# Two-layer DiT block in fp32 on one core: modulation steps of the FFN two to a tile, three chunks moved to layer 1's projections, later stores, a second norm row buffer, early first splits of the down projection

## The chip, the cores and the metric

The kernel runs on one core of a Trainium2 chip. A time is the device time of one execution, in microseconds; of several runs the median is given. PE is TensorE, DVE VectorE, ACT ScalarE, POOL GpSimd, and SP is SyncE, which here issues nearly all transfers.

## The reference, cut to what matters

Two layers over 1024 tokens and 256 context tokens of width 1024, all in fp32. Layer 0 mixes a gated recurrence with an attention over latent keys, layer 1 is a differential attention. Around them:

```python
for li in range(2):
    mod = silu(c) @ w_mod[li] + b_mod[li]
    mod_c = silu(c_ctx) @ w_mod[li] + b_mod[li]
    sh1, sc1, ga1, sh2, sc2, ga2 = split(mod, 6)
    u = rmsnorm(h, g_norm1[li]) * (1 + sc1) + sh1
    y, yc = mixer(u, uc)
    h = h + ga1 * y
    u = rmsnorm(h, g_norm2[li]) * (1 + sc2) + sh2
    a, g = split(u @ w_up[li], 2)
    h = h + ga2 * ((gelu(dwconv(g)) * a) @ w_down[li])
    # layer 0 does the same for the context with mod_c
```

## The kernel before, in words

Every fp32 product is three matmuls of rounded parts, hi·hi, lo·hi and hi·lo (`mm3`, L116 to L118). An operand is split by an ACT copy (L283, hi) and a DVE subtraction (L98, lo), for some weights by POOL instead (L90). The stages in order, with their places in the span: layer 0's front and mixer to about 740, its output projection (`out_proj`) to 857, the start of its FFN (`begin0`, `up_sequence`) to 909, the up projection's tiles to 1492.6, the down projection (`ffn_down`) to 1845.6, layer 1's projections (`layer1_front`) to 2185, the differential attention, output projection 1 to 2717, layer 1's up projection to 3177 and its down projection to the end.

**Modulation.** The 12 columns of 512 of `w_mod` of a layer are chunks. A chunk in `mod_chunk_dve` is a generator of six steps that other code calls one at a time: (1) POOL clears the sum, `b_mod` is loaded into its first row, the first 512 KB piece of `w_mod` is requested; (2) to (5) DVE adds two products of that piece per context (L194, `macc<-wr,sc,macc`; four instructions with two contexts, two with one), and SP requests the next piece into the same single buffer; (6) PE sums over the partitions with matmuls one column wide (`modps`, L204, or L211 for the gates) and DVE copies the result out.

**Up projection** (`up_sequence`). The 2816 hidden columns are 22 tiles of 128; a tile is a seven-product scheme over halves of the operands (products "11", "t2", "t1", "t3", "21", "t4", "22" into the PSUM banks B, E, A, and C for the context). The order of the code is the order of the engines here. In each pass the previous tile is finished: DVE takes the gate, convolves it (L930 to L932), multiplies it by the other half (L1118, `gc`) and SP stores it in `hid` (L1119). `some_mods()` runs a modulation step in one slot after product t1 (a second one there, if there are more than two a tile) and one after `second(X)`. The last piece of a chunk is thus added in the first slot and summed by PE in the second. Layer 0 has nine chunks here: four and two of two contexts, three of one.

**Down projection** (`ffn_down`). Rounds of 4, 3 and 3 token tiles (layer 1: 4 and 4), 22 items a round, one for each 128 hidden columns. An item's weights `wr` and hidden rows `hr` are requested three items ahead (`fetch`), split one item ahead (`split`) and multiplied into `acc`. At a round's end DVE multiplies `acc` by the gate `ga` (L1235, `dtmp`) and POOL adds it to the residual (L1236). One extra step per item or so follows: in layer 0's rounds 1 and 2 the 18 steps of chunks 7 to 9 of layer 1, then the norm of finished token tiles for layer 1 (`columns`, three steps each: Square on ACT with the rstd chain of POOL's pow and DVE's L130 to L133; PE's transposes `ntp` with DVE's and ACT's `v`; the split to `u`).

**Output projection.** Items are staggered: load, product, and the norm some items later, in one row buffer `xn`, which takes the Square's output first and the normed row later, and which PE's transposes read.

**Layer 1's projections.** 56 items (block, token tile) in the block order 4, 2, 3, 0, 1, 5, staggered with lags; here a planner places instructions by its own time model within each engine's queue. Three token tiles that the down projection leaves are loaded, scaled (lag 4) and normed (lag 7) early. Blocks 0 to 3 end with a norm, the rotation and four transposes whose result goes out as `dk` or `dq` (L1336, 128 KB each).

## Time and profile before

| | us |
|---|---|
| median of 3 runs | 3421.39 |
| lowest and highest run | 3420.65, 3423.81 |
| the profiled execution's own time | 3431.7 |
| its span | 3429.9 |
| PE, DVE, ACT, POOL busy | 3186.3, 2360.9, 1412.1, 945.2 |
| mean granted clock of PE | 0.974 |

Times in rows count from the span's start. A table of stretches gives for each stretch its length, each engine's busy time with its instructions, then the granted clock of PE (1.00 is the level of 2.4 GHz, 0.5 that of 1.2 GHz, between them a mixture), the busy share of the DMA engines and GB/s. In a timeline the bracket tells how long the engine was idle before the row, and what released it. A wait row reads: engine, what waited, what it waited for, then the total, the times and the longest.

### The profile page before, as it was taken

To read this page: it belongs to the slowest core of one execution; us is meant where nothing else is said; L and a number is where in the kernel's file an instruction comes from. 1 tells how busy PE (TensorE), PEld (TensorE's weight loads), DVE (VectorE), ACT (ScalarE), POOL (GpSimd) and SP (SyncE) were. 2 spreads that over 40 slices of the span, in tenths; PEclk is the share of its full clock that TensorE was granted. 3 is DMA by queue.
4 is the path that set the end of the run, shared out by engine and by line. 5 is a ranking of instruction groups with operands and counts; after the bars stand their busy time and mean duration, and the time that the engine had idled before them with its cause. 6 is when DMAs were issued, how large, how long until landed. Compare 5 with 4: busy or idle time off the path is not lost.

```text
span 3429.9 us, 43450 instructions
## 1 busy us (share of the span) xinstructions
PE 3186.3 (93%) x16262; PEld 2633.3 (77%) x16262; DVE 2360.9 (69%) x3381; ACT 1412.1 (41%) x2444; POOL 945.2 (28%) x654
## 2 busy tenths in 40 slices
PE   8998889989799999989899999888888889999998
PEld 4777778878578778868777887777777768888887
DVE  6468978855776777643566687599997687666443
ACT  3355766733422223322243222477763333333322
POOL 2223578864000000000122223277764200000010
PEclk9999999999899999999999999999999999999999
DMA  6224953344122223234755355444414122223553
GB/s 261 70 77 129 285 141 94 89 137 134 47 96 97 97 97 111 97 123 151 249 192 182 120 139 131 146 114 126 111 62 160 62 86 101 90 74 98 181 180 124
DMA packets 232298, 434.07 MB, mean 127 GB/s; under 512 B 21484, under 2 KB 147692, under 8 KB 230296
## 3 DMA queue, kind: packets, MB, share of 16 engines
q1 hardware_dynamic: 230216, 424.49, 39.3%
q10 hardware_dynamic: 1872, 6.82, 0.6%
q8 instruction: 128, 2.10, 0.2%
q14 instruction: 82, 0.67, 0.1%
HBM read 319.89 MB, written 111.34 MB: 126 GB/s over the span
## 4 chain that ended last, share of the span: by engine, by line
PE 54%; DVE 14%; DMA 3%; issue 3%; ACT 3%; POOL 1%; SPq 0%; DVEq 0%; ACTq 0%; POOLq 0%
PE acc L118 4%; PE pB L116 4%; PE pB L118 4%; PE pB L117 4%; PE acc L116 4%; PE acc L117 4%; DVE m L1456 3%; PE pj L116 3%; PE pj L117 3%; PE pj L118 3%; DVE p L1472 3%; PE pE L118 2%; PE pE L116 2%; PE pE L117 2%; PE ops L117 2%
## 5 line engine op out<-in xcount | busy, mean ns | idle before, releaser
L98 DVE TENSOR_TENSOR wl<-wr,wh 128x1024 fp32r<-128x1024 f32 (+2 forms) x285 | 348.8, 1233 | 92.9 <-ACT wh L283 63.4
L116 PE MATMUL acc<-wh,hh 128*128 128x512 f32 x792 | 312.5, 395 | 18.7 <-ACT wh L283 17.1
L118 PE MATMUL acc<-wl,hh 128*128 128x512 f32 x792 | 312.5, 395 | 9.6 <-DVE wl L98 8.9
L117 PE MATMUL acc<-wh,hl 128*128 128x512 f32 x792 | 310.6, 392 | 4.5 <-DVE hl L98 4.5
L1236 POOL TENSOR_TENSOR ht<-ht,dtmp 128x1024 f32<-128x1024 f32 x17 | 45.7, 2715 | 857.1 <-DVE dtmp L1235 857.1
L283 ACT CAST wh<-wr 128x1024 fp32r<-128x1024 f32 (+1 forms) x221 | 220.9, 1008 | 83.4 <-DVE wr L999 72.4
L98 POOL TENSOR_TENSOR wl<-wf,wh 128x1280 fp32r<-128x1280 f32 x64 | 221.9, 3468 | 106.3 <-ACT wh L1491 94.7
L1451 PE MATMUL S<-k,q 128*128 128x512 f32 (+1 forms) x768 | 197.8, 382 | 55.7 <-ACT p L1462 55.5
L116 PE MATMUL pB<-ht,wh 128*128 128x512 f32 x528 | 210.4, 398 | 16.5 <-ACT ht L283 6.5
L98 DVE TENSOR_TENSOR hl<-hr,hh 128x512 fp32r<-128x512 f32 (+1 forms) x110 | 76.0, 691 | 206.7 <-ACT hh L283 206.6
L118 PE MATMUL pB<-lt,wh 128*128 128x512 f32 x528 | 210.3, 398 | 2.2 <-DVE lt L98 2.0
L117 PE MATMUL pB<-ht,wl 128*128 128x512 f32 x528 | 209.5, 397 | 0.8 <-DVE wl L98 0.8
L194 DVE SCALAR_TENSOR_TENSOR macc<-wr,sc,macc 128x512 f32<-128x512 f32 x192 | 135.8, 748 | 105.2 <-DMA wr<-w_mod 104.1
L283 ACT CAST hh<-hr 128x512 fp32r<-128x512 f32 (+1 forms) x110 | 63.7, 579 | 325.0 <-PE acc L118 242.0
L1462 ACT ACTIVATE p<-S,m 128x1280 f32<-128x1280 f32 x128 | 170.8, 1334 | 60.6 <-DVE m L1456 57.5
L1456 DVE TENSOR_REDUCE m<-S 128x1 f32<-128x1280 f32 x128 | 187.1, 1479 | 6.2 <-PE S L1451 5.6
L116 PEld LDWEIGHTS acc<-wh,hh 128*128 128x128 f32 x792 | 149.8, 189 | 53.4 <-ACT wh L283 21.8
L177 POOL MEMSET macc<- 128x512 f32 x24 | 12.4, 526 | 636.8 <-PE modps L211 283.3
L118 PEld LDWEIGHTS acc<-wl,hh 128*128 128x128 f32 x792 | 149.7, 189 | 49.4 <-DVE wl L98 18.6
L1451 PEld LDWEIGHTS S<-k,q 128*128 128x128 f32 x768 | 124.9, 193 | 77.2 <-ACT p L1462 64.5
L116 PE MATMUL pj<-wh,u 128*128 128x512 f32 x448 | 177.6, 396 | 2.5 <-DVE qT L98 2.5
L117 PE MATMUL pj<-wh,u 128*128 128x512 f32 x448 | 178.0, 397 | 0.0
(414 smaller groups left out, 9178.3 us busy)
## 6 DMA issues: line engine op xcount, KB each, us to landing
wr<-ffn_down SPq DMA_DIRECT2D x110, 512.0 KB
wr<-ffn_up SPq DMA_DIRECT2D x90, 512.0 KB
wr<-w_mod SPq DMA_DIRECT2D x76, 512.0 KB
hid<-gc SPq DMA_DIRECT2D x44, 512.0 KB
k<-dk SPq DMA_DIRECT2D x14, 1280.0 KB
hr<-hid SPq DMA_DIRECT2D x66, 256.0 KB
wr<-w_in_c SPq DMA_DIRECT2D x24, 512.0 KB
mr<-w_mod SPq DMA_DIRECT2D x20, 512.0 KB
```

The lines of the kernel that those rows point to most:

```text
L98: e.tensor_tensor(out, x, hi.bitcast(F32), op=SUB)
L116: mm(out, a[0], b[0], start=start, stop=False, skip_group_check=onto)
L117: mm(out, a[1], b[0], start=False, stop=False, skip_group_check=onto)
L118: mm(out, a[0], b[1], start=False, stop=stop, skip_group_check=onto)
L177: nc.gpsimd.memset(acc[c], 0.0)
L194: nc.vector.scalar_tensor_tensor(acc[c], raw[:, kk * 512:(kk + 1) * 512], self.sc[:, 2 * u + kk, c:c + 1], acc[c], op0=MUL, op1=ADD)
L283: self.nc.scalar.copy(hi, x)
L1236: (nc.vector if last else nc.gpsimd).tensor_tensor(hts[t][:, c], hts[t][:, c], tmp[:, c], op=ADD)
L1451: nc.tensor.matmul(Y["S", m][:, c0:c0 + n], heads[h]["q"][m][:, t * P:(t + 1) * P], heads[h]["k"][x, m, j], start=(x == 0), stop=(x == 1))
L1456: nc.vector.tensor_reduce(Y["m", m], Y["S", m][:, :TOK], axis=AX.X, op=ALU.max, negate=True)
L1462: nc.scalar.activation(Y["p", m], Y["S", m][:, :TOK], AF.Exp, bias=Y["m", m], accum_out=Y["s"] if m else s0[:, h, t:t + 1])
L1472: nc.vector.scalar_tensor_tensor(Y["p", 0], Y["p", 1], Y["tt"], Y["p", 0], op0=MUL, op1=ADD)
```

## The change

1. `up_sequence`: two steps a tile, one in each slot; the third call goes. Layer 0's list has six chunks of two contexts (36 steps for 18 tiles); layer 1's chunks 4 to 6 leave it, 7 to 9 leave the down projection, and all six run in `layer1_front`, one step for each item outside block 4 (`mod`, lag 5).
2. The store of `hid` goes out after `second(X)`, half a tile later, but for the last tile.
3. `fetch_down` requests the first down item's operands in tile 20, and tile 21 splits them (`self.ahead`); `ffn_down` begins with them. The gate rows `ga` are requested at item 4.
4. `norm` in `out_proj` has two `xn` buffers. Room for it: one `cgc` buffer, a smaller DMA scratch, and W's split tiles all 1024 wide.
5. The start of the up projection splits "t2" before it copies out the first product (`p1_out`; in layer 1 there is nothing to copy).
6. In `layer1_front` the early scale and norm come one item later.

```diff
--- before.py
+++ after.py
@@ -828,7 +828,7 @@
...
-                xn = O.tile([P, D], F32, tag="xn", bufs=1, name="xn")
+                xn = O.tile([P, D], F32, tag="xn", bufs=2, name="xn")
                 junk = xn.rearrange("p (k c) -> p k c", c=P)
@@ -919,7 +919,7 @@
...
         n = x.shape[-1]
-        hi, lo = ((pool or self.W).tile([P, n], F32R, tag=tag + y, bufs=bufs, name="w" + y) for y in "hl")
+        hi, lo = ((pool or self.W).tile([P, n if pool else 1024], F32R, tag=tag + y, bufs=bufs, name="w" + y)[:, :n] for y in "hl")
         self.split(x, hi, lo)
@@ -946,7 +946,7 @@
...
         nc.scalar.copy(self.cg[:, 1:1 + CTX], pg)
-        gc = F.tile([P, CTX], F32, tag="cgc", bufs=2, name="gc")
+        gc = F.tile([P, CTX], F32, tag="cgc", bufs=1, name="gc")
         self.convolved(0, f, self.cg, gc, CTX)
@@ -1073,8 +1073,8 @@
...
         p1(X)
+        self.split_columns(U, "t2")
         p1_out(X)
-        self.split_columns(U, "t2")
         p6(X)
@@ -1101,7 +1101,6 @@
...
         mods += [x for ch in chunks for x in self.mod_steps(F, *ch)]
-        per = -(-len(mods) // (NF - 2))
         for f in range(1, NF + 1):
@@ -1116,8 +1115,8 @@
...
             nc.vector.tensor_mul(gc, gc, Y["sum"])
-            nc.sync.dma_start(self.hid_d[f - 1, :, :SEQ], gc)
             if f == NF:
+                nc.sync.dma_start(self.hid_d[f - 1, :, :SEQ], gc)
                 break
@@ -1127,8 +1126,6 @@
...
             some_mods()
-            if per > 2:
-                some_mods()
             if here:
@@ -1138,6 +1135,7 @@
...
             second(X)
+            nc.sync.dma_start(self.hid_d[f - 1, :, :SEQ], gc)
             some_mods()
@@ -1150,8 +1148,18 @@
...
                 raws = self.fetch_up(l, f + 2)
-        while mods:
-            some_mods()
+            elif f + 2 == NF:
+                raws = self.fetch_down(l)
+            else:
+
+                self.ahead = self.split_new(raws[1]), self.split_new(raws[0])
+        assert not mods
+
+    def fetch_down(self, l):
+        w, x = (self.W.tile([P, 1024], F32, tag="wr", bufs=NWR, name="wr") for _ in range(2))
+        self.nc.sync.dma_start(w, self.io["ffn_down"][l, :P, :])
+        self.nc.sync.dma_start(x[:, :512], self.hid_d[0, :, :512])
+        return w, x[:, :512]
@@ -1163,7 +1171,6 @@
...
             F = self.sb(st, f"down{l}")
-            gas = [self.ga(F, l, 1, c, f"ga{c}") for c in range(2 if l == 0 else 1)]
             extra = []
@@ -1196,9 +1203,9 @@
...
             with self.tc.manual_schedule():
-                for i in range(3):
+                parts[0] = self.ahead
+                for i in range(1, 3):
                     fetch(i)
-                split(0)
                 for r, tiles in enumerate(rounds):
@@ -1211,6 +1218,8 @@
...
                                 fetch(i + 3)
+                            if i == 4:
+                                gas = [self.ga(F, l, 1, c, f"ga{c}") for c in range(2 if l == 0 else 1)]
                             if f == 8:
@@ -1338,13 +1347,19 @@
...
                 self.heads = {}
+                mods = [step for ch in range(4, 10) for step in self.mod_steps(M, 1, ch, 1)]
+
+                def mod(item):
+                    if mods and item[0] != 4:
+                        mods.pop(0)()
...
                 early = (lambda f: lambda item: f(item[1] + n0) if item[0] == 4 and item[1] + n0 < NT else None)
-                self.staggered(items, (early(load), 0), (early(scale), 4), (early(norm), 7), (project, 4), (finish, 5), (first_head, 8))
+                self.staggered(items, (early(load), 0), (early(scale), 5), (early(norm), 8), (project, 4), (finish, 5), (mod, 5), (first_head, 8))
+                assert not mods
@@ -1628,10 +1643,10 @@
...
                     self.out_proj(0, "w_out_ab", [*range(NTX, NT), *range(NTX)], self.yT0, lambda: self.begin0(F0))
-                self.ffn_up(0, F0, [(1, ch, 2) for ch in range(4)] + [(0, ch, 2) for ch in (10, 11)] + [(1, ch, 1) for ch in range(4, 7)])
+                self.ffn_up(0, F0, [(1, ch, 2) for ch in range(4)] + [(0, ch, 2) for ch in (10, 11)] + [])
                 self.ctx_columns.close()
             columns = st.enter_context(ExitStack())
-            self.ffn_down(0, [range(0, 4), range(4, 7), range(7, NT)], lambda t: self.h1_d[t], range(7, 10), columns)
+            self.ffn_down(0, [range(0, 4), range(4, 7), range(7, NT)], lambda t: self.h1_d[t], (), columns)
             with ExitStack() as s2:
@@ -1708,7 +1723,7 @@
...
     arrays = layout({k: np.asarray(v) for k, v in inputs.items()})
-    nc = bacc.Bacc("TRN2", target_bir_lowering=False, num_devices=1, dynamic_dma_scratch_size=1024)
+    nc = bacc.Bacc("TRN2", target_bir_lowering=False, num_devices=1, dynamic_dma_scratch_size=512)
     io = {k: nc.dram_tensor(k, v.shape, F32, kind="ExternalInput").ap() for k, v in arrays.items()}
```

The order on SP where layer 0's up projection ends and its down projection begins, before:

```order
L1178 DMA wr<-ffn_down 128x1024
L1119 DMA hid<-gc 128x1024
L955 DMA hid<-gc 128x256
L1119 DMA hid<-gc 128x1024
L955 DMA hid<-gc 128x256
L1119 DMA hid<-gc 128x1024
L244 DMA ga<-ga_132 128x1024
L244 DMA ga<-ga_133 128x1024
L1181 DMA hr<-hid 128x512
L1178 DMA wr<-ffn_down 128x1024
L1181 DMA hr<-hid 128x512
```

and with the change:

```order
L915 DMA wr<-ffn_up 128x1024 x2
L1138 DMA hid<-gc 128x1024
L955 DMA hid<-gc 128x256
L1160 DMA wr<-ffn_down 128x1024
L1161 DMA wr<-hid 128x512
L1185 DMA wr<-ffn_down 128x1024
L1138 DMA hid<-gc 128x1024
L955 DMA hid<-gc 128x256
L1119 DMA hid<-gc 128x1024
L1188 DMA hr<-hid 128x512
```

The first down weights and hidden rows (L1160, L1161) now stand two tile stores ahead, the two `ga` loads are gone from here, and the request of item 1's rows (L1188) stands directly behind the last store.

DVE at the first items of round 1 of layer 0's down projection (`hl`, `wl` are an item's split rows and weights), before, from the round's end on, and one item later:

```order
L1235 TENSOR_TENSOR dtmp<-acc,ga 128x1024 x4
L98 TENSOR_TENSOR hl<-hr,hh 128x384
L98 TENSOR_TENSOR wl<-wr,wh 128x1024
L98 TENSOR_TENSOR hl<-hr,hh 128x384
L98 TENSOR_TENSOR wl<-wr,wh 128x1024
L194 SCALAR_TENSOR_TENSOR macc<-wr,sc,macc 128x512 x2
L98 TENSOR_TENSOR hl<-hr,hh 128x384
L98 TENSOR_TENSOR wl<-wr,wh 128x1024
L194 SCALAR_TENSOR_TENSOR macc<-wr,sc,macc 128x512 x2
```

and with the change:

```order
L1244 TENSOR_TENSOR dtmp<-acc,ga 128x1024 x4
L98 TENSOR_TENSOR hl<-hr,hh 128x384
L98 TENSOR_TENSOR wl<-wr,wh 128x1024
L258 TENSOR_SCALAR ss<-ss 128x1
L130 TENSOR_TENSOR rs_t<-rs_y 128x1
L131 TENSOR_TENSOR rs_t<-rs_t,ss 128x1
L132 TENSOR_SCALAR rs_t<-rs_t 128x1
L133 TENSOR_TENSOR rs_y<-rs_y,rs_t 128x1
L98 TENSOR_TENSOR hl<-hr,hh 128x384
L98 TENSOR_TENSOR wl<-wr,wh 128x1024
L273 TENSOR_SCALAR v<-ntp,A,B 128x128 x5
```

The accumulations L194 between the items' splits are gone; the rstd chain (`ss`, `rs_t`, `rs_y`) and the transposes' evacuation `v` of the first token tile's norm stand in their place.

SP in block 2 of layer 1's projections, before:

```order
L105 DMA wr<-w_in_c 128x1024
L1336 DMA dk<-qT 256x1x128 x28
L105 DMA wr<-w_in_c 128x1024 x2
L1336 DMA dk<-qT 256x1x128 x2
L105 DMA wr<-w_in_c 128x1024
L1336 DMA dk<-qT 256x1x128 x6
L105 DMA wr<-w_in_c 128x1024
L1336 DMA dk<-qT 256x1x128 x28
```

and with the change:

```order
L1345 DMA dk<-qT 256x1x128 x20
L214 DMA ga_134<-mrow 1x512
L178 DMA macc<-b_mod 1x512
L183 DMA wr<-w_mod 128x1024
L1345 DMA dk<-qT 256x1x128 x4
L183 DMA wr<-w_mod 128x1024
L1345 DMA dk<-qT 256x1x128 x4
L183 DMA wr<-w_mod 128x1024
L105 DMA wr<-w_in_c 128x1024 x3
```

The loads of `w_mod` (L183) stand one by one between the stores `dk` of successive items.

## Rows read from the trace of the kernel before

**Rows 1.** The page's first part: busy us, share of the span, instructions.
```profile
PE 3186.3 (93%) x16262; PEld 2633.3 (77%) x16262; DVE 2360.9 (69%) x3381; ACT 1412.1 (41%) x2444; POOL 945.2 (28%) x654
```

**Rows 2.** Stretches of layer 0's up projection, with the view's heading.
```profile
core 0: us, PE busy (x) PEld busy (x) DVE busy (x) ACT busy (x) POOL busy (x), PEclk, DMA share, GB/s
932.60:1281.20 348.60, 329.14 (x1658) 277.21 (x1656) 254.44 (x352) 96.12 (x145) 5.78 (x11) 0.95 0.28 97
969.95:994.90 24.95, 24.95 (x134) 21.26 (x133) 13.61 (x19) 6.40 (x11) 0.00 (x0) 1.00 0.33 111
994.90:1027.60 32.70, 30.16 (x151) 26.14 (x150) 27.12 (x38) 9.03 (x15) 1.05 (x2) 0.90 0.25 85
1281.20:1459.40 178.20, 178.20 (x939) 150.15 (x938) 127.07 (x169) 56.55 (x85) 1.06 (x2) 1.00 0.29 100
```

**Rows 3.** Timeline, DVE, one such tile: start us, us, operation [idle before <-releaser].
```profile
1011.62 2.73 DVE L194 SCALAR_TENSOR_TENSOR macc<-wr,sc,macc 128x512 f32<-128x512 f32 x4
1017.70 2.74 DVE L194 SCALAR_TENSOR_TENSOR macc<-wr,sc,macc 128x512 f32<-128x512 f32 x4 [3.35 <-DMA wr<-w_mod]
```

**Rows 4.** Stretches at the seam from layer 0's up to its down projection.
```profile
1492.60:1505.90 13.30, 0.17 (x1) 0.00 (x0) 4.07 (x5) 2.62 (x3) 0.00 (x0) 0.60 0.65 221
1505.90:1514.70 8.80, 8.74 (x24) 6.51 (x25) 4.88 (x5) 3.13 (x4) 0.00 (x0) 0.63 0.79 255
1514.70:1520.20 5.50, 5.50 (x26) 4.53 (x26) 1.92 (x2) 1.57 (x2) 0.00 (x0) 1.00 0.52 168
```

**Rows 5.** Timeline, ACT, at the same seam.
```profile
1504.31 0.62 ACT L283 CAST hh<-hr 128x512 fp32r<-128x512 f32 x1 [9.02 <-DMA hr<-hid]
```

**Rows 6.** Stretches of layer 0's down projection: rounds 1, 2; four items; three.
```profile
1629.00:1739.80 110.80, 99.42 (x430) 78.08 (x428) 65.84 (x93) 35.97 (x52) 14.30 (x11) 0.97 0.66 234
1739.80:1845.60 105.80, 99.94 (x444) 77.90 (x445) 66.82 (x116) 46.65 (x76) 26.47 (x17) 1.00 0.55 181
1668.60:1684.90 16.30, 16.30 (x73) 13.51 (x72) 6.21 (x8) 4.39 (x6) 0.00 (x0) 1.00 0.83 308
1766.10:1780.60 14.50, 13.71 (x63) 10.78 (x63) 8.49 (x18) 7.19 (x13) 2.87 (x2) 1.00 0.47 150
```

**Rows 7.** Timeline, DVE, start of round 1.
```profile
1631.51 3.41 DVE L98 TENSOR_TENSOR wl<-wr,wh 128x1024 fp32r<-128x1024 f32 x1
1645.53 1.54 DVE L194 SCALAR_TENSOR_TENSOR macc<-wr,sc,macc 128x512 f32<-128x512 f32 x2 [6.82 <-DMA wr<-w_mod]
1650.87 1.54 DVE L194 SCALAR_TENSOR_TENSOR macc<-wr,sc,macc 128x512 f32<-128x512 f32 x2 [2.20 <-DMA wr<-w_mod]
```

**Rows 8.** Timeline, POOL, start of round 1.
```profile
1626.40 10.76 POOL L1236 TENSOR_TENSOR ht<-ht,dtmp 128x1024 f32<-128x1024 f32 x4 [270.13 <-DVE dtmp L1235]
```

**Rows 9.** Waits of PE, 855 to 908: us in total, times, longest.
```profile
PE ntp L270 <- POOL xn L260: 9.4, 1, 9.4
PE pB L116 <- ACT ht L283: 1.6, 1, 1.6
```

**Rows 10.** Waits of PE, 2700 to 2760 (end of output projection 1).
```profile
PE ntp L270 <- POOL xn L260: 7.4, 1, 7.4
PE pB L116 <- ACT ht L283: 4.8, 1, 4.8
```

**Rows 11.** Waits of PE, 3170 to 3195 (layer 1, up to down).
```profile
PE acc L118 <- DVE wl L98: 1.3, 1, 1.3
```

**Rows 12.** Timeline, ACT, end of output projection 0.
```profile
858.16 1.06 ACT L257 ACTIVATE xn<-tmp 128x1024 f32<-128x1024 f32 x1 [2.02 <-PE ntp L270]
```

**Rows 13.** Waits of PE, 1845.6 to 1900 (start of layer 1's front).
```profile
PE ntp L270 <- DVE rs_t L130: 4.3, 1, 4.3
```

**Rows 14.** One stretch of layer 1's front (blocks 2, 3, 0, 1).
```profile
1929.00:2145.00 216.00, 212.56 (x991) 172.97 (x990) 163.03 (x385) 47.04 (x103) 73.32 (x73) 1.00 0.49 127
```

**Rows 15.** Timeline, DVE, second context gate of `begin0`.
```profile
881.89 0.41 DVE L930 TENSOR_SCALAR gc<-cg,cols 128x256 f32<-128x256 f32 x1 [2.23 <-ACT cg L948]
```

**Rows 16.** Waits of SP's DMA queue, 1900 to 2160.
```profile
SPq L1336 <- ACT qT L393: 92.0, 24, 12.8
```


## Prediction

> **What bounds the kernel now.** I read the page's busy times first, then a table of stretches along the span, then the waits of PE at each seam, then DVE's and SP's own waits. PE is busy for 93% of the span [rows 1], so a saving must come from PE's idle gaps, from the slow matmuls that follow them, or from matmuls not issued; no matmul leaves. The places are these.
>
> Layer 0's up projection: a tile without a finishing modulation step takes 24.95 us at clock 1.00; one in which a two-context chunk finishes takes 32.70 at clock 0.90, PE idle for 2.54 of it [rows 2]. Why: DVE does the third accumulation, waits 3.35 us for the next piece of w_mod (one buffer, so it was requested only then), does the fourth [rows 3], and PE stands in order before the small modps matmuls that read the sum. Later finishes of one context, half the accumulations, stop nothing: three in seven tiles cost 178.20 − 7 × 24.95 = 3.55 [rows 2].
>
> The seam to layer 0's down projection: PE idle 13.3, then item 0 takes 8.8 at clock 0.63 where item 1 takes 5.5 [rows 4]; ACT had waited 9.02 us for hr [rows 5]. Rounds 1 and 2 of that projection take 110.8 and 105.8 [rows 6], where four clean items take 16.3, so 22 take 89.7. The ends of both output projections wait for xn, 9.4 and 7.4 us [rows 9, 10]. Layer 1's front stands once, 4.3 us, for its early norm [rows 13]. There, over 216 us, PE is idle for 3.4 and DVE for 53 [rows 14].
>
> **The change, part by part** (saved: minus).
>
> *Up tiles.* The twelve tiles from 932.6 take 348.6, over the base by 348.6 − 299.4 = 49.2; with the 3.55 above, 52.7 are modulation's [rows 2]. After: two steps a tile in two slots, so the fourth accumulation stands half a tile (12 us) after its load and half a tile before modps. The six finishes left, all two-context, cost their matmuls: twice 3.55/3, 2.4 each, 14.2. **−38.5**; ends −25 (half the stalls stay) and −40. The hid store now goes out after `second(X)`, half a tile later; its buffer is written again a full tile after the old place, so half a tile is left to it: nothing. If that cover were gone, DVE's next convolution, and PE's pE sum behind it, would wait for one store in each tile. On SP the store changes places with the first slot's w_mod load, and neither waits for long there.
>
> *Seam to down.* Before, item 1 ends at 1520.2. Item 0's operands are now split during the last tile, so item 0 goes straight on: 1492.6 to 1498.1. Item 1's hr is still behind the last hid store on SP, which waits for DVE's product (about 1496.5, a little after ACT's wait began [rows 5]); the two ga loads no longer stand between. Before, hr came 7.8 us after that point; without the ga loads I take 4 to 5, the splits 1: PE goes on at 1502.5 after a gap of 4.4, and its slow start costs 3.3 as before. Item 1 ends near 1511.3: **−8.9**, ends −5 and −12. Layer 1's seam, whose first operands are split early too, waits only 1.3 for wl [rows 11]: **−1.5** with the matmuls after it.
>
> *Down, rounds 1 and 2.* The 18 steps of three chunks leave. DVE stood up to 6.82 us for w_mod here [rows 7], with the next item's hl and wl queued behind it and PE waiting for those. Over the clean time are 21.1 and 16.1. The norm columns that stay cost (14.5 − 12.2) = 2.3 a token tile [rows 6], 9.1 in round 1 and 6.8 in round 2. They now begin at the first item, where POOL still adds for 10.76 us [rows 8]: rs_t waits behind those adds, DVE's splits behind rs_t; I leave 5 a round for it, near the 4 PE lost at the old start. 37.2 − 15.9 − 10 = 11.3: **−11**, ends −16 and −4. The row beside POOL's adds: wl takes 3.41 us there [rows 7]. The Trainium skill, *GPSIMD Engine Reference*, "Key points", says why: GpSimd shares its SBUF interfaces with VectorE and contends with instructions that have two SBUF inputs; the trace agrees for that row. By that rule the accumulations, two-input as well, stretch wherever POOL works.
>
> *Output projections.* With one xn, the Square of the next tile waits for PE's transposes of this one [rows 12] and the whole norm follows. With two it runs as soon as its input is there, before PE's last products; from the Square's start at 858.16 to PE's going on at the end of the 9.4 are some 9.3 us, all of which can lie beside those products. But DVE's part of the chain is queued among splits that wait for ffn_up's loads, so I take 6.8 of the 9.4: **−6.8** (−4 to −9). In layer 1, with no context work and fewer splits there, **−6** (−4 to −8) of the 7.4 and the 4.8 behind it [rows 10]: the last tile's chain runs earlier too. What is late next is that last tile's norm.
>
> *Small ones.* split_columns before p1_out takes the 1.6 before pB [rows 9]: **−1.4** (0 to −2). One cgc buffer: in begin0 the second gate starts 2.23 us after DVE was free [rows 15]; the store in between may outlast that: **+0.5** (0 to +3). The Trainium skill, *Trainium Kernel Development and Optimization*, "Best Practices", says to double-buffer, which speaks against this edit; by the rule the sum would be up to 2.5 worse. Early norm one item later: **−5**: the 4.3 [rows 13] and most of a slow restart, by the 3.3 after the longer gap at the seam (0 to −6.5).
>
> *Layer 1's front, what is added:* 24 loads of 512 KB, 24 times two accumulations, six finishes. The finishes on PE cost 3.55/3 each [rows 2], 7.1. DVE: a pair takes about 1.5, as the row of 1645.53 [rows 7]; 24 pairs at 1.45 without the overlap of successive instructions are 34.8 of the 53 us idle; 18 are left for waits on loads. The loads stand in SP's queue between the dk and dq stores, and SP waited there 24 times, 92.0 us, for ACT's qT [rows 16]. A load has one item, 6 us; in down the whole cycle of such a step took 5.3, from 1645.53 to 1650.87 [rows 7], so most arrive in time. DVE at nine tenths will make PE wait at the weight splits: +7 (0 to +23). **+14**, ends +7 and +30.
>
> *No cost:* w tiles of one width, the smaller DMA scratch, ga at item 4: SBUF room and loads not needed before a round's end.
>
> Sum: −38.5 −8.9 −1.5 −11 −6.8 −6 −1.4 +0.5 −5 +14 = **−64.6**. The span of 3429.9 becomes 3365. The runs' median is 3421.4, 10 below the profiled execution's 3431.7; I take the change off the median: **3357**. What can be told from no change is about 0.2%, 7 us.
>
> **Rivals.**
> 1. *DVE becomes the bound in layer 1's front.* POOL works 73 of 216 us there [rows 14]; stretched accumulations and late loads fill all 53 us and more: +35 instead of +14. For: 34.8 of 53 gone. Against: POOL's work there is small tiles. 3378; 14%.
> 2. *Down's rounds wait for POOL instead of w_mod.* rs_t at the first item costs as much as the chunks did, 0 instead of −11, and the seam gives only −5: 3372. Against: one start a round, not four chunks. 10%.
> 3. *The up projection keeps its stalls.* If the slots stand closer than half a tile on DVE, six finishes still lose 2.5 and the slow stretch after, 5.8 each beyond the matmuls: +35 on the sum, 3392. Against: rows 3 show the wait starting with the request, and the request moves. 5%.
> 4. *Slower than before.* Each w_mod load of the front is issued behind a store that waits for ACT's qT, ACT's qT waits for PE, PE for DVE, DVE for the load: a ring that costs PE a stop per load. It decides against the change from 24 loads × 3.3 = 79 us on, the sum without the front's cost; with the 2.5 idle and 3.3 slow of the up tiles, 24 × 5.8 = 139: 3421 − 79 + 139 = 3481. For: SP's 92.0 us. Against: those waits were harmless, as the loads queued with them had slack. 3%.
>
> **How the numbers follow.** Forecast 68%, rivals 14, 10, 5 and 3. The good ends of all terms together give −90, the bad ones without a rival about −40; the range takes most of rivals 1 and 2 in: 3330 to 3386. Faster by over 0.2%: all but rival 4 and a mixture of the others with bad ends: 0.94; within 0.2%: 0.02; slower 0.04.
>
> **What would show it.** Right: no tile of layer 0's up projection over 27.6 us, clock 1.00 through them; item 0 of down starting within 1 us of the last up matmul, then one gap of 3 to 6 before item 1; rounds near 104 and 102; ntp of the output projections after 3 us or less; DVE in layer 1's front near 94% with L194 waits on w_mod under 1 us each. Wrong: DVE macc waits over 40 us in the front with PE gaps beside them (rivals 1, 4); rs_t waits over 5 us a round (2); modps matmuls with an idle time before them (3).

## The result, and the profile with the change

The change takes 3380.63 us (median of 4 runs, 3376.81 to 3381.11); the kernel before took 3422.2 beside it (4 runs). The ratio is 0.9876, 95% interval 0.9859 to 0.9893, so 42 us are saved: the forecast's sign, inside its range, but 24 above its 3357. The two profiled executions stand 54.9 apart (spans 3429.9 and 3375.0), since the first lies 9.5 above its median and the second 3.8 below; stage by stage:

| stage | before | change | difference | forecast |
|---|---|---|---|---|
| start to the last product of output projection 0 | 857.2 | 854.7 | −2.5 | untouched |
| from there to the first up matmul | 30.1 | 24.8 | −5.3 | −6.8 + 0.5 |
| layer 0's up projection with its start | 605.5 | 560.9 | −44.6 | −38.5 − 1.4 |
| seam and round 0 of down | 136.2 | 126.8 | −9.4 | −8.9 |
| rounds 1 and 2 | 216.6 | 204.0 | −12.6 | −11 |
| layer 1's front | 339.9 | 363.1 | **+23.2** | **+14 − 5** |
| attention, products of output projection 1 | 531.4 | 533.5 | +2.1 | untouched |
| from there to the first up matmul | 23.2 | 18.1 | −5.1 | −6 |
| layer 1's FFN | 689.8 | 689.1 | −0.7 | −1.5 |
| sum | | | −54.9 | −64.6 |

One row is off by much: the front. First the places that went as forecast. The page's first part [rows 1]: PE lost 24.9 us of busy time with the same 16262 matmuls, so slow ones became fast (mean granted clock 0.974 before, 0.982 now).

```profile
PE 3161.4 (94%) x16262; PEld 2615.9 (78%) x16262; DVE 2368.7 (70%) x3381; ACT 1411.5 (42%) x2444; POOL 951.7 (28%) x654
```

Stretches of layer 0's up projection, columns as in [rows 2]: a plain tile, a tile with a two-context finish, and all tiles but the last.

```profile
973.10:998.00 24.90, 24.90 (x134) 21.20 (x133) 14.71 (x19) 7.48 (x12) 0.00 (x0) 1.00 0.26 90
1023.00:1049.80 26.80, 26.80 (x150) 23.12 (x149) 21.76 (x33) 8.62 (x13) 1.05 (x2) 1.00 0.24 84
897.40:1432.00 534.60, 530.96 (x2798) 448.79 (x2797) 395.18 (x529) 174.52 (x257) 6.25 (x12) 1.00 0.26 90
```

The finishing tile has no idle PE and its clock stays at 1.00; it costs 1.9 over a plain one, not 7.75 [rows 2]. The same tiles together were 575.6 before, so 41.0 leave. DVE's timeline in two such tiles [rows 3]: the four-instruction accumulations stand 10.8 and 14.1 us apart (the one before these at 1012.81; 6.1 apart in [rows 3]) and have no bracket, so w_mod is there in time.

```profile
1023.65 2.74 DVE L194 SCALAR_TENSOR_TENSOR macc<-wr,sc,macc 128x512 f32<-128x512 f32 x4
...
1037.77 2.73 DVE L194 SCALAR_TENSOR_TENSOR macc<-wr,sc,macc 128x512 f32<-128x512 f32 x4
```

The seam [rows 4] and rounds 1 and 2 [rows 6]: the early first item, the gap, item 1, then the rounds.

```profile
1440.30:1445.80 5.50, 5.50 (x25) 4.29 (x23) 3.29 (x4) 1.06 (x1) 0.00 (x0) 1.00 0.15 59
1445.80:1449.70 3.90, 0.08 (x1) 0.00 (x0) 0.69 (x1) 1.56 (x2) 0.00 (x0) 0.91 0.94 322
1449.70:1458.40 8.70, 8.64 (x25) 6.40 (x26) 4.97 (x5) 3.13 (x4) 0.00 (x0) 0.65 0.95 312
1567.20:1670.00 102.80, 96.14 (x430) 76.84 (x428) 58.13 (x92) 43.36 (x68) 20.85 (x12) 1.00 0.57 191
1670.00:1771.20 101.20, 96.18 (x422) 77.42 (x421) 58.37 (x88) 39.28 (x60) 18.94 (x13) 0.98 0.57 189
```

Item 0 follows the last up matmul at once. A gap of 3.9 and a slow item 1 (clock 0.65) follow, since its hidden rows are still behind the last store; ACT waits 5.21 for them instead of 9.02 [rows 5]:

```profile
1448.11 0.62 ACT L283 CAST hh<-hr 128x512 fp32r<-128x512 f32 x1 [5.21 <-DMA hr<-hid]
```

PE's waits at the ends of output projections 0 (850 to 905) and 1 (2660 to 2710), against [rows 9, 10]:

```profile
PE pB L116 <- DVE gc L954: 7.6, 1, 7.6
PE ntp L270 <- POOL xn L260: 1.7, 1, 1.7
```
```profile
PE pB L116 <- ACT ht L283: 4.8, 1, 4.8
PE ntp L270 <- DVE xn L260: 4.0, 1, 4.0
```

The wait for xn fell from 9.4 to 1.7 and another of 1.2, and from 7.4 to 4.0. In the first place PE then stands 7.6 for the context's gate sum (5.1 before), which is late next.

Now the front: the whole of it, and two pairs of items (token tiles) at the start of blocks 3 and 1. Items are counted from 0 in the order of the blocks, so the pairs are 20 and 21, 38 and 39 of the 56. Blocks 2, 3, 0 and 1 of [rows 14] lie in it; as a stretch of their own they are the first row.

```profile
1855.00:2090.00 235.00, 217.73 (x1002) 174.37 (x1001) 195.62 (x425) 45.17 (x100) 82.35 (x77) 0.97 0.56 155
1771.00:2134.00 363.00, 342.38 (x1550) 275.81 (x1548) 254.47 (x531) 70.85 (x146) 108.70 (x97) 0.98 0.55 166
1894.10:1913.50 19.40, 14.17 (x57) 11.05 (x56) 17.69 (x35) 2.47 (x6) 4.08 (x4) 0.82 0.74 217
2017.00:2037.70 20.70, 14.04 (x57) 10.70 (x55) 19.85 (x36) 3.35 (x7) 9.62 (x8) 0.84 0.33 102
```

DVE is busy for 91% and 96% of the pairs, PE idle for 5 to 7 us, and the clock falls behind the idle time. Before, the pairs took 12.1 and 13.4:

```profile
1968.40:1980.50 12.10, 12.10 (x57) 9.80 (x57) 11.81 (x24) 2.64 (x6) 1.05 (x1) 1.00 0.74 214
2077.40:2090.90 13.50, 12.56 (x58) 9.78 (x57) 13.36 (x28) 2.79 (x6) 2.65 (x3) 1.00 0.46 117
```

DVE was busy for 98% and 99% of them even then, yet PE stood for only 0 and 0.9 us. What PE waited for with the change, 1771 to 2135, and for qT in the same stage before:

```profile
PE pj L116 <- DVE qT L98: 14.5, 5, 6.0
PE pj L116 <- ACT v L275: 2.4, 1, 2.4
```
```profile
PE pj L116 <- DVE qT L98: 2.5, 2, 1.5
```

And what DVE waited for on w_mod:

```profile
DVE macc L194 <- DMA wr<-w_mod: 8.0, 8, 1.6
```

Eight waits, 1.6 us at most: the loads are hardly late, and rival 4's ring isn't there. What holds qT is DVE's own queue. DVE, start of block 3, with the change, then the same place before:

```profile
1899.68 0.74 DVE L194 SCALAR_TENSOR_TENSOR macc<-wr,sc,macc 128x512 f32<-128x512 f32 x1
1900.34 0.68 DVE L1336 TENSOR_TENSOR qo<-qn,g 128x512 f32<-128x512 f32 x1
1900.94 1.22 DVE L98 TENSOR_TENSOR wl<-wr,wh 128x1024 fp32r<-128x1024 f32 x1
1902.07 1.02 DVE L1328 TENSOR_SCALAR ms<-ms 128x8 f32<-128x8 f32 x1
1903.00 0.74 DVE L194 SCALAR_TENSOR_TENSOR macc<-wr,sc,macc 128x512 f32<-128x512 f32 x1
1903.66 1.21 DVE L98 TENSOR_TENSOR wl<-wr,wh 128x1024 fp32r<-128x1024 f32 x1
...
1905.46 0.68 DVE L98 TENSOR_TENSOR qT<-pj,qT 128x512 fp32r<-128x512 f32 x1
```
```profile
1970.15 0.68 DVE L1327 TENSOR_TENSOR qo<-qn,g 128x512 f32<-128x512 f32 x1
1970.75 2.35 DVE L98 TENSOR_TENSOR wl<-wr,wh 128x1024 fp32r<-128x1024 f32 x2
1973.02 0.68 DVE L1318 TENSOR_REDUCE ms<-sq 128x8 f32<-128x512 f32 x1
1973.62 0.68 DVE L98 TENSOR_TENSOR qT<-pj,qT 128x512 fp32r<-128x512 f32 x1
1974.21 0.83 DVE L1319 TENSOR_SCALAR ms<-ms 128x8 f32<-128x8 f32 x1
1975.06 1.23 DVE L98 TENSOR_TENSOR wl<-wr,wh 128x1024 fp32r<-128x1024 f32 x1
```

From qo to qT it was 3.47 us and is 5.12, and the rows before it run late too (qn, at 1968.41, stood level with the item's start before; at 1898.48 it stands 4.4 behind it): the item's PE time grew from 6.5 to 12.1. The planner fits accumulations, the next block's weight splits (wl) and small norm steps into a queue that was full here already, and qT comes late by what stands ahead of it.

The third new place is the early norm, which the planner now runs among accumulations: the first chunk's were placed into block 4. DVE there, and ACT, which stands for a store (dv) of split values:

```profile
1792.02 0.75 DVE L194 SCALAR_TENSOR_TENSOR macc<-wr,sc,macc 128x512 f32<-128x512 f32 x1
...
1794.19 0.68 DVE L98 TENSOR_TENSOR vst<-pj,vst 128x512 fp32r<-128x512 f32 x1
```
```profile
1799.48 0.59 ACT L283 CAST vst<-pj 128x512 fp32r<-128x512 f32 x1 [7.01 <-DMA dv<-vst]
```

SP issues the store at 1794.90, right after the split (1794.19 + 0.68), and ACT goes on 4.6 later. ACT's longest such wait was 2.7 before. In items 0 to 7 the front gained 1.1 (53.6 to 52.5), not 5: the stall left item 2 and came back in items 4 to 6 (9.16 for item 5).

So +23.2 is made of: −1.1 in items 0 to 7; the six finishes 6.6; the pairs above 7.4 and 7.3 over before; items 30 to 32 about 2.6; the rest, about 0.5, is spread.

### The profile page after: what moved, and what is told of

It reads as the page before. It is cut to its first block, busy times and chain, and to the rows that moved or that the text cites. A ratio compares the mean times of both kernels' runs of the same rounds, so it can differ in the third digit from the quotient of the medians.

```text
span 3375.0 us, 43426 instructions
## 1 busy us (share of the span) xinstructions
PE 3161.4 (94%) x16262; PEld 2615.9 (78%) x16262; DVE 2368.7 (70%) x3381; ACT 1411.5 (42%) x2444; POOL 951.7 (28%) x654
## 4 chain that ended last, share of the span: by engine, by line
PE 56%; DVE 13%; issue 5%; ACT 2%; DMA 2%; POOL 1%; SPq 0%; DVEq 0%; ACTq 0%; POOLq 0%
PE pB L116 5%; PE pB L118 5%; PE pB L117 5%; PE acc L118 4%; PE acc L116 4%; PE acc L117 4%; DVE m L1471 3%; PE pj L116 3%; DVE p L1487 2%; PE pj L117 2%; PE pj L118 2%; PE pE L118 2%; PE pE L116 2%; PE pE L117 2%; PE S L1466 2%
## 5 line engine op out<-in xcount | busy, mean ns | idle before, releaser
L118 PE MATMUL acc<-wl,hh 128*128 128x512 f32 x776 | 304.8, 393 | 7.7 <-DVE wl L98 7.6
L116 PE MATMUL acc<-wh,hh 128*128 128x512 f32 x776 | 305.4, 394 | 5.8 <-ACT wh L283 5.8
L1245 POOL TENSOR_TENSOR ht<-ht,dtmp 128x1024 f32<-128x1024 f32 x17 | 44.7, 2660 | 919.2 <-DVE dtmp L1244 919.2
L117 PE MATMUL acc<-wh,hl 128*128 128x512 f32 x776 | 303.7, 391 | 0.0
L116 PE MATMUL pj<-wh,u 128*128 128x512 f32 x448 | 180.7, 403 | 17.8 <-DVE qT L98 14.5
L118 PEld LDWEIGHTS acc<-wl,hh 128*128 128x128 f32 x776 | 146.6, 189 | 43.1 <-DVE wl L98 12.8
L118 PE MATMUL pj<-wl,u 128*128 128x512 f32 x448 | 178.0, 398 | 0.0
L1037 ACT COPY g<-pB 128x512 f32<-128x512 f32 x84 | 49.6, 590 | 304.9 <-PE pB L118 304.9
```

Of the source, the lines that this page charges most:

```text
L116: mm(out, a[0], b[0], start=start, stop=False, skip_group_check=onto)
L117: mm(out, a[1], b[0], start=False, stop=False, skip_group_check=onto)
L118: mm(out, a[0], b[1], start=False, stop=stop, skip_group_check=onto)
L1037: nc.scalar.copy(out, x)
L1245: (nc.vector if last else nc.gpsimd).tensor_tensor(hts[t][:, c], hts[t][:, c], tmp[:, c], op=ADD)
```

## The experiments

Three theories of the front's +23 stood against each other: the order of DVE's queue at block starts; POOL's work slowing DVE; and mere amount of work on DVE. Beside them stood the question why the up projection gained. Each kernel is compared with the kernel before run beside it on the same chip, 3428.61 to 3430.16 there (median). Where two changed kernels are compared by their times, the runs can be of different sets.

**The kernel before, once more**, since its first trace lies 9.5 above its median.

> The kernel before, unchanged, for a second trace. The profiled execution of before took 3431.7, 9.5 above its runs' median of 3422.2; the changed kernel's took 3376.8, 4 below its own. Theory A (the first trace caught a slow execution; the change is worth what the runs say, about 42): a second trace takes 3420 to 3424, and the 10 us are missing in one place that waits for DMA, most likely the finishing tiles of layer 0's up projection (49.2 over the base in the first trace, about 40 in the second) or the seam to the down projection. Theory B (a profiled execution of this kernel is always slower): 3430 to 3433 again, with the same tiles at the same lengths.

3428.61 (3427.32 to 3433.26), ratio 1.000 (0.999 to 1.0009); span 3428.8, all stages within 3 us of the first trace. Neither expectation holds: no place has the 9.5, and this trace lies only 2 above the median of its own runs. The level differs between sets of runs, 3422 and 3429, and single executions spread by some us. Where the 9.5 lay stays open. The change once more, beside such runs:

> The changed kernel, unchanged, timed beside the others: the reference for them, since the kernel before took 3428.9 on the chip of the first experiments and 3422.2 on that of the result. Theory (the difference is the chip's): 41 to 48 below the kernel before, and the same stalls in layer 1's front at the starts of blocks 3 and 1 (19.4 and 20.8 us for two items). Rival (the front's stalls come and go with transfers): another total for the front than 363, by over 4 us.

3379.62 (3376.67 to 3381.99), 0.986 (0.9845 to 0.9874), −49; span 3374.9, front 365.2, and the same two pairs stall (19.8 and 23.0). So the stalls belong to the program, not to one execution.

**Modulation steps of the front kept away from block starts.**

```diff
-                    if mods and item[0] != 4:
+                    blk, t = item
+                    first, last = {4: (5, 9), 5: (0, 9), 2: (2, 7), 3: (2, 7), 0: (2, 6), 1: (2, 6)}[blk]
+                    if mods and first <= t <= last:
```

> The changed kernel, with layer 1's front calling a modulation step only for items at which DVE has room: block 4 from its item 5, blocks 2 and 3 at items 2 to 7, blocks 0 and 1 at 2 to 6, and all of block 5. Theory (the front lost 24 us more in its items 7 to 47 because the accumulations meet the weight splits at block starts: items 20 and 21 took 19.4 instead of 12.1, 38 and 39 20.8 instead of 13.4): these two places fall back to 12 to 14 each, the front takes 12 to 16 us less, about 3367. Rival (any accumulation in the front delays PE, since DVE's order is full): no change within 4 us, 3377 to 3384.

3381.27 (3375.88 to 3385.14), 0.9858 (0.9844 to 0.9873): no gain, front 364.6. Block starts still stall (items 20 and 21 take 15.9, 38 and 39 19.2), though no accumulation stands inside them, and DVE is busy for 93% and 99% of them. DVE, start of block 3:

```profile
1897.30 1.21 DVE L98 TENSOR_TENSOR wl<-wr,wh 128x1024 fp32r<-128x1024 f32 x1
...
1899.04 1.21 DVE L98 TENSOR_TENSOR wl<-wr,wh 128x1024 fp32r<-128x1024 f32 x1
...
1900.24 0.68 DVE L98 TENSOR_TENSOR qT<-pj,qT 128x512 fp32r<-128x512 f32 x1
```

All four weight splits now stand ahead of qT (the first two at 1889.68 and 1894.72); before, the fourth came behind it. DVE enters the block start already late (qn at 1894.11 stands 1.8 behind the item's start), and a stall moved even to block 5 (item 49, 10.5). The narrow form of the theory, accumulations at the start itself, falls; the rival, that any accumulation here delays PE, is left standing.

**Three chunks back in the down projection** (the front keeps three).

```diff
-                mods = [step for ch in range(4, 10) for step in self.mod_steps(M, 1, ch, 1)]
+                mods = [step for ch in range(4, 7) for step in self.mod_steps(M, 1, ch, 1)]
...
-            self.ffn_down(0, ..., lambda t: self.h1_d[t], (), columns)
+            self.ffn_down(0, ..., lambda t: self.h1_d[t], range(7, 10), columns)
```

> The changed kernel with chunks 7 to 9 back in layer 0's down projection; the front keeps chunks 4 to 6. Theory (the front loses more than 3 us a chunk, of which the block starts take most, and the down projection lost about 12 to three chunks): rounds 1 and 2 of the down projection go from 204 back to 212 to 217, the front from 363 to about 350; 3378 to 3384, no gain or loss. Rival (the front is cheap, and only two block starts that happen to collide cost): the front stays over 358 and the time rises to 3388 to 3393.

3381.99 (3378.8 to 3384.27), 0.9861 (0.9846 to 0.9876): as the change. Rounds 1 and 2 take 217.2 (+13), the front 355.7 (9.5 less than the change's second trace). By the traces three chunks are dearer in the down projection than in the front; the times don't tell the two apart. DVE's w_mod wait in its rounds is back, 35.4 in 12 waits.

**Weight rounding of the front on ACT, not POOL.**

```diff
-self.unit(io["w_in_c"][blk, w], pool=M if order.index(blk) % 2 else None)
+self.unit(io["w_in_c"][blk, w], pool=M if order.index(blk) % 2 else None, heng="a")
```

> The changed kernel with the rounding of layer 1's front weights on ACT instead of POOL. Theory (beside POOL's rounding DVE's accumulations take 1.4 to 1.6 instead of 0.74 and its small statistics 0.7 to 1.0 instead of 0.15; that is what fills DVE at the block starts): DVE's busy time in the front falls by 8 to 15 us and the front from 363 to 365 to 350 to 357. Rival (the order of DVE's queue, with the fourth weight split before qT, is the cause; ACT's queue gets the casts in its way): the front stays over 360.

3374.44 (3373.23 to 3376.14), 0.984 (0.9825 to 0.9854), some 5 better than the change. The front:

```profile
1771.00:2134.00 363.00, 346.61 (x1554) 279.25 (x1553) 238.96 (x532) 92.07 (x168) 83.59 (x76) 0.98 0.55 166
```

DVE's work is the same (532 instructions, 531 with the change) and takes 15.5 us less with 25 us less of POOL. The Trainium skill, *GPSIMD Engine Reference*, "Key points", names that contention; the trace agrees. But the stage is hardly shorter (361.8), and items 39 and 40 still take 11.0 and 10.6. So POOL does slow DVE, and giving DVE that time back didn't shorten the front. How much of the +23 is POOL's isn't settled by it, since ACT got 21 us more work: block 3's first pair fell to 16.8, and at items 38 to 40 DVE is busy for only 21.9 of 29.8 us and waits 6.1 for ACT's qT, a stall of another kind.

**A third step a tile in the up projection**, a second buffer for the pieces of w_mod (`mr`), four more chunks there; the front keeps two, in blocks 2 and 3.

```diff
-                self.ffn_up(0, F0, ... + [])
+                self.ffn_up(0, F0, ... + [(1, ch, 1) for ch in range(4, 8)])
...
             product(X["B"], X["g"], 512, "t4", False)
+            if l == 0:
+                some_mods()
```

> The changed kernel with a third step at the end of each tile of layer 0's up projection, two buffers for the pieces of w_mod, and ten chunks there instead of six; layer 1's front keeps chunks 8 and 9, at items 2 to 7 of blocks 2 and 3. Theory (three steps a tile stalled only because they stood together; the front is the dear place): up tiles stay under 28 us at clock 1.00, the ten finishes cost about 17 instead of 12, the front falls from 363 to 342 to 347; 11 to 17 us less than the changed kernel. Rival (a third set of accumulations is too much for DVE in a 25 us tile): tiles of 26 to 30 us, the up projection 20 us longer or more, no gain in all.

3364.54 (3359.28 to 3370.82), 0.9817 (0.9802 to 0.9832), 15 better than the change. The front takes 345.0, and the up projection 565.8 with 60 steps instead of 36; no tile takes over 26.98, the clock stays at 1.00. So with two buffers three steps a tile cost their matmuls alone when each has its own slot; with one buffer that wasn't run. The early stall grew: the planner still put accumulations into block 4, and ACT waits 9.01 for the store.

**All twelve chunks in the up projection, none in the front**: three slots a tile, 35 of them with one step, then two and one by turns; two mr buffers; then the same with the early norm at its old lags.

```diff
-                self.ffn_up(0, F0, ... + [])
+                self.ffn_up(0, F0, ... + [(1, ch, 1) for ch in range(4, 10)])
...
+        mods += [1] * 35 + [2, 1, 2, 1] * 6 + [1] if l == 0 else [1] * len(steps)
```
```diff
-(early(scale), 5), (early(norm), 8)
+(early(scale), 4), (early(norm), 7)
```

> The third-slot kernel (three steps a tile in layer 0's up projection, two buffers for the pieces of w_mod) with all twelve chunks in the up projection: 36 steps of the two-context chunks one a slot, then the 36 of the one-context chunks one or two a slot, a finishing step never behind an accumulation of its own slot. Layer 1's front has no modulation. Theory (the front's loss, its early norm included, is the modulation's: hoisted w_mod loads stand before the dv stores on SP, and accumulations meet the weight splits): ACT's waits for dv stores at the front's start are back under 3 us, the front takes 333 to 338 (third-slot kernel 345, changed 363 to 365, before 340), two more finishes cost 2.4 in the up projection; 6 to 10 us less than the third-slot kernel, about 3356. Rival (the early norm's lag is itself the cause of the stall at items 4 and 5): that stall of 9 us stays, 3360 to 3366.

> The same as the kernel with all twelve chunks in the up projection, with the early scale and norm at lags 4 and 7, as before the change. Theory (one item later was worth 5 us): 4 to 6 us more, PE waiting 4 us before the first ntp. Rival (the later start of the down projection's last stores and loads makes the lags equal): within 2 us.

3354.97 (3351.82 to 3359.12), 0.9783 (0.9767 to 0.9799), and 3351.27 (3349.19 to 3354.97), 0.9775 (0.9757 to 0.9793): the best versions, not told apart, 75 and 79 below the kernel before. The up projection takes 568 and 567, 6 to 7 more than the change's; the front 333.7 and 335.2, 28 to 30 less. Items 8 to 47 take 241.6 and 241.4, where they took 241.4 before and 265.8 with the change: what the front lost there is the modulation's. ACT's longest wait for a dv store was 4.7 in the first, where under 3 had been expected; from the split's end to ACT's going on it took 3.0, where the change takes 4.6 with w_mod loads beside it. PE's waits, old lags:

```profile
PE pj L116 <- DVE qT L98: 2.4, 2, 1.5
PE ntp L270 <- DVE rs_t L130: 1.5, 1, 1.5
```

Those are the waits before the change, but for ntp, 1.5 where it had been 4.3 [rows 13]. So the later lag itself is worth some 1.5 of the front, which the two times don't show; the 4 to 6 expected of it weren't there. Most of the old 4.3 left without the lag: ACT's longest wait for the early tiles' x was 4.1 before and is 1.6 here.

**Two mr buffers in the kernel before** (and one buffer, cgc, for the context's gate).

```diff
-tag="mr", bufs=1
+tag="mr", bufs=2
...
-tag="cgc", bufs=2
+tag="cgc", bufs=1
```

> The kernel before with two buffers for the pieces of w_mod instead of one (and one cgc buffer, for room); the three steps a tile, all nine chunks of layer 1 and the down projection's three stay where they were. Theory (the finishing tiles stall since the fourth piece is requested only after the third is added): the wait of 3.35 on DVE goes, PE's 2.5 before modps and the slow stretch after go with it, the six two-context finishing tiles fall from 31 to 37 to about 27.5; 3385 to 3395 with the down projection's stalls smaller too. Rival (three steps are too many for DVE in a tile; the count is the cause): the tiles stay over 30 and the time over 3410.

3407.75 (3404.03 to 3410.48), 0.9936 (0.9921 to 0.9951), −21; 13.5 of it in the up projection, the rest in the down projection and the front. The finishing tiles still take 28.5 to 35.1, and DVE's wait hardly falls in sum, before and with two buffers:

```profile
DVE macc L194 <- DMA wr<-w_mod: 67.4, 18, 4.3
DVE macc L194 <- DMA wr<-w_mod: 61.9, 18, 5.0
```

So a buffer gives less than a third of the 44.6. The rest is the spacing of the steps and, with some 3.6 [rows 2], the three one-context finishes that left. But the buffer couldn't show its full worth: in the tile at 991 SP sent the request of the fourth piece at 1008.09, right behind the store of hid, which waits for DVE's product `gc`. DVE began the third accumulation at 1008.16, and the fourth waited 1.65 (3.35 in [rows 3], with the request at 1014.38, behind the third). Two buffers with the later store and the old slots weren't run.

**One part taken back at a time.** One xn buffer:

```diff
-                xn = O.tile([P, D], F32, tag="xn", bufs=2, name="xn")
+                xn = O.tile([P, D], F32, tag="xn", bufs=1, name="xn")
```

> The changed kernel with one xn buffer in the output projections, as before. Theory (the Square had to wait for PE's transposes, and the second buffer is worth 5 us at each of the two ends): the ends go from 24.8 and 18.1 back to about 30 and 23, 10 us more in all. Rival (the shorter ends come from the earlier split of t2 and from layer 1's planner): under 3 us more.

3390.1 (3387.68 to 3396.02), 0.9893 (0.9878 to 0.9908): 10.5 worse than the change. The waits of [rows 9] are back, and at the second end 7.4 [rows 10]; the first end of its trace:

```profile
PE ntp L270 <- POOL xn L260: 9.4, 1, 9.4
PE pB L116 <- DVE gc L954: 5.1, 1, 5.1
```

No early split, in both layers (the ga loads again at the down projection's start, as before):

```diff
-                self.ahead = self.split_new(raws[1]), self.split_new(raws[0])
...
-                parts[0] = self.ahead
+                split(0)
```

> The changed kernel without the first down splits in the up projection: requests of items 0 to 2 and the gate rows at the start of the down projection, item 0 split there. Theory (the seam gains by item 0 alone; item 1's rows still come behind the last store): up to item 2 the seam goes back by 9 to 10 us in layer 0 and 1 to 2 in layer 1, 10 to 12 in all. Rival (half of it is the gate rows' place in the queue): the gap before item 0 is 11 to 13.2 as before and nothing else changes, 8 in all.

3392.37 (3391.44 to 3393.99), 0.9898 (0.9882 to 0.9915): 12.8 worse. Layer 0's seam and round 0 take 9.9 more, and PE's wait at the seam is 14.5 in one piece.

The hid store at its old place:

```diff
+            nc.sync.dma_start(self.hid_d[f - 1, :, :SEQ], gc)
             if f == NF:
-                nc.sync.dma_start(self.hid_d[f - 1, :, :SEQ], gc)
                 break
...
-            nc.sync.dma_start(self.hid_d[f - 1, :, :SEQ], gc)
```

> The changed kernel with the store of hid where it was, before the next tile's first slot. Theory (half a tile of cover on both sides): within 3 us of the changed kernel in the up projections, no wait on DVE's convolution. Rival (the store's place moves the w_mod load behind it on SP, which made the stall): up tiles over 28 us, 5 us or more.

3381.11 (3379.91 to 3382.95), 0.9859 (0.9844 to 0.9874): as the change, all up tiles the same. With the steps spaced, the later store does nothing, neither good nor harm.

## Why the prediction was right, and where it failed

- *Up tiles*, −38.5: right, −41.0. A finish costs 1.9 to 2.0, not 2.4; all stalls left, as "the wait starting with the request, and the request moves" had it. The longest tile is 26.95, under the 27.6 named. The run with three steps a tile sharpens the cause: the number of steps isn't it. The prediction laid the late request to the one buffer; with two it still stood behind the store of hid. Rival 3 falls.
- *Seam to down*, −8.9: right, −9.4; the gap was 3.9 where 4.4 stood, the slow item 3.2 over a clean one where 3.3 stood. The run without the early split is 12.8 slower, 9.9 of it here; the two ga loads' place is in that sum.
- *Down, rounds 1 and 2*, −11: right; "near 104 and 102" were 102.8 and 101.2. Rival 2's waits, DVE's for POOL's rs_y, came to 6.7 in seven over both rounds, and the rounds ended within the 5 each left for them.
- *Output projections*, −6.8 and −6: nearly right, −5.3 and −5.1; by the run with one xn buffer 10.5 for both. The sign "ntp of the output projections after 3 us or less" held at the first, not at the second (4.0). In the first the gate sum took over, 7.6 where the run with one xn buffer has 5.1; that one also has one cgc buffer, so the longer wait isn't the cgc edit's. The rule of the Trainium skill, *Trainium Kernel Development and Optimization*, "Best Practices", to double-buffer, which the prediction held against one cgc buffer, was worth nothing there; for xn a second buffer was worth 10.5.
- *Small ones*, −1.4 and +0.5: no run shows them alone. From the first up matmul to the first tile of the stretch of tiles above it took 21.5 before, 17.9 with the change and 19.0 with one xn buffer.
- *Layer 1's front, what is added*, +14: **the step that failed**, in its last term: "DVE at nine tenths will make PE wait at the weight splits: +7". The finishes were 6.6 for 7.1; the waits about 17. What DVE had to do was priced well: in blocks 2, 3, 0 and 1 it is busy for about 33 us more, where 34.8 stood. But the spare 53 us of DVE was taken as one sum over 216 us. It isn't one: at block starts, where four weight splits fall in, DVE is busy for over 90% before, with the change and with the accumulations kept away, and what it brings along late ends on PE twice, as idle time and as the slow clock behind it (0.82 and 0.84 in the pairs). So the stage grew longer instead of DVE fuller: the sign "near 94%" came out as 83% (195.6 of 235.0), and the longest w_mod wait as 1.6, not under 1. Rival 1, the same mechanism priced at +35, was about as far off (+24.4 in items 8 to 47, halfway between). Of its two causes, loads were not late (8.0 in all); with less POOL work (rounding on ACT) DVE had 15.5 us back and the stage 1 to 3, and how large a part the stretched operations have isn't settled. Whether the order of DVE's queue or the mere amount of work in it makes the stalls isn't separated; that the steps moved here make them is shown by the run without any.
- *Early norm*, −5: failed as well, −1.1. The term took the stall for a matter of one item's lag; it came back as ACT's wait for a store that DVE's split sends late, behind accumulations, and that lands later (how much is which isn't shown). Without any steps there (all chunks in the up projection) no early stall is left with the new lag, and 1.5 with the old one.
- The 23.6 between 3357 and 3380.6: the two failed terms together, forecast +9 and measured +23.2, are 14.2; the other stages came out 4.5 better by the traces; 13.3 are the distances of the two traces from their medians (9.5 and 3.8), since the sum was made against one trace and laid on a median; the median before was 0.8 higher this time. That 3380.6 still fell into the range is owed to its width, which had rival 1 in it. By medians the change saves 42 beside its own runs and 49 in another set; what sets the level of a set wasn't found.
- Not tried: the front's block starts in an order set by hand, and what part of the early stall is the split's and what the store's landing.

## What to carry to other kernels

Give an accumulation, the load it frees and PE's read of the sum each a slot of its own, a good part of a tile apart; with a second buffer even three steps a tile then cost nothing here but their matmuls. A second buffer alone helps only as far as the request isn't queued behind something else. Before background work is moved into a stage, look at its fullest stretches on the engine that does it, not at the idle time of the whole stage; a stall on PE cost twice here, once as idle time and once as the slow clock after it.

## What the runs showed of the hardware

- DVE's smallest operations (128x8) take 0.15 to 0.2 us alone and up to 1.0 where POOL works beside them, and L194 1.41 to 1.61 instead of 0.74. DVE beside POOL's L90 and L387:

```profile
1892.49 1.41 DVE L194 SCALAR_TENSOR_TENSOR macc<-wr,sc,macc 128x512 f32<-128x512 f32 x1
...
1895.25 0.98 DVE L132 TENSOR_SCALAR rs_t<-rs_t 128x8 f32<-128x8 f32 x1
```

- The same kernel took 3422 us beside the change's first runs and 3429 to 3430 in the experiments' sets of runs.
